# One step of a two-layer RWKV-7 and differential-attention trunk: the order of small products in quarters of the array, of the output projection, and of the memory keys

## The chip, the core and the metric

The kernel is one program on one core of a Trainium2 chip. The metric is the device time of one execution in microseconds (us). The engines are named as in the profile: PE (matrix products) and PEld (its weight loads), DVE (vector), ACT (scalar, activations and copies), POOL (general), SP (which issues the DMAs here). Each engine works through its own queue in order; semaphores tie the queues together.

## What is computed

Layer 0 mixes tokens with RWKV-7, layer 1 with differential attention. Each layer is a norm, one input projection, a mixer, a cross-attention over 256 memory rows (4 heads), a gate, one output projection and a residual add. Shapes: 512 prompt tokens and 32 sample tokens (544 columns in all), width 1024, 24 RWKV heads of 64, branch width 2048. All in float32.

```python
def rwkv_layer(x, mk, mv, prev_row, S0, norm_w, w_out, w_in, ...):
    h = rmsnorm(x, norm_w)
    p, qm, gate = jnp.split(h @ w_in, [RW_PROJ, RW_PROJ + MEM_W], axis=-1)
    y_mix, S_T, last_row = rwkv_mixer(p, prev_row, S0, ...)
    y_mem = mem_attention(qm, mk, mv)
    out = jnp.concatenate([y_mix, y_mem], axis=-1) * jax.nn.silu(gate)
    return x + out @ w_out, S_T, last_row

# in rwkv_mixer, for every token:
    sa = jnp.einsum('bhvk,bhk->bhv', S, -kk_t)
    S = S * w_t[:, :, None, :] + sa[..., None] * (kk_t * a_t)[:, :, None, :] + v_t[..., None] * k_t[:, :, None, :]
    y = jnp.einsum('bhvk,bhk->bhv', S, r_t)
# then a group norm of y per head, plus sum(r * k * r_k) * v
```

Layer 1 has the same frame, with `diff_layer` in the mixer's place. For each layer the memory rows are also normed and multiplied by `w_mem_k` and `w_mem_v` (outputs too).

## The kernel before

**Projections.** Activations lie with the feature on the 128 partitions and the 544 tokens along the free axis. A float32 product is made of three single-pass ones: activation and weight are each split into a rounded part and a rest (`hh`/`hl`, `whi`/`wlo`), and `hh*whi`, `hl*whi`, `hh*wlo` are summed in PSUM (tile `ps_g`). I call these *main products*; one takes 128 x 272. A weight block is 1024 x 128: `load` issues two DMAs into `raw` (5 buffers), `split` lets ACT make `whi` and DVE `wlo` (2 buffers each), and 48 main products use it. Products of plain float32 tiles (all others) appear in the trace as two records each, transposes as one.

**Layer 0** works on 12 pairs of heads. For each pair: `rw_prep` (decays, scaled keys, the 64 x 64 triangles `at` of nine chunks: eight of 64 tokens, and the sample), `rw_invert` on POOL (inverts 32 x 32 triangles, 62 small instructions, after a round trip through DRAM), `rw_back` and `rw_at` (the inverses come back by DMA), `rw_merge` (two rounds of sixteen 32 x 32 products, tile `ps_w`, join the inverses to 64 x 64), `rw_values` (64 x 64 products, tile `ps_v`), the recurrence `rw_chain` (23 steps, each a product `ps_c`, then DVE or ACT, then the next), `rw_outputs` (`ps_yc`), and `rw_finish` (the group norm `fin`: sums, square on ACT, an inverse root by eight small DVE instructions, five transposes `ps_y`, the gate, then a DMA of the gated block `sg` to the scratch tensor `oscr`).

**Order in layer 0.** It is written by hand. `Queue.tie` makes every engine keep the order in which the program names its instructions, while `ordered` is set. `FILL0` to `FILL3` give the opening (pairs 0 to 2 prepared between main products). Then for each pair `PLAN` has 23 rows of two halves: after each step of the recurrence it names what else is issued there, for the pair itself (0), the next (1), the ones after (2, 3) or the last (-1). Main products of the `blocks` list fill in between (192 in a usual pair). ACT and DVE work for the weight blocks waits in `later` and is issued one piece at a time by `some`. `MPLAN` does the same for the steps of the memory cross-attention in pairs 10 and 11.

**End of layer 0.** After pair 11's recurrence, its `rw_outputs` and `rw_finish` stand between the main products of `w_mem_k` of layer 1. Then `ordered` is off, and the framework's scheduler orders the rest: `w_out` fetches sixteen gated blocks from `oscr` into `os`, splits each into `hi` (ACT) and `lo` (DVE), and multiplies: eight output blocks `k`, each with two weight blocks `q`, each with two token halves, 24 main products in each. The residual comes in as products of raw rows of `x` with the identity into the same PSUM tile (`extra`, 48 products). ACT copies the sum to `x1` and squares it. `token_rms` and eight rounds of DVE, ACT and POOL (`hn`, `hh`, `hl`) then give layer 1's normed input, while PE multiplies `w_mem_v`.

**PSUM pools:** `psg` 3 banks (main products), `psm` 2, `psx` 1, `psc` 2 (recurrence).

**Layer 1** goes over 12 heads in three groups, with main products from `proj` and `gate`, and then `w_out` again, with the gated blocks in SBUF (`og`).

Of the kernel before, what the change touches and what calls it, by code (L numbers as in the profile page):

```python
# [2 lines left out]

# [5 lines left out]
F32 = mybir.dt.float32  # L9
# [7 lines left out]
P = 128  # L17
D = 1024
# [20 lines left out]
OSB = 4  # L39
# [4 lines left out]
LATER = 0.75  # L44
PLAN = [
    [[("val", 0, 1.1, 0), ("prep", 2, 0.1, 0)], [("prep", 2, 0, 0.42)]],
    [[("val", 0, 0.8, 0)], []],
    [[("prep", 1, 0.53, 0)], [("prep", 1, 0, 0), ("prep", 2, 0, 1.04)]],
    [[("prep", 2, 0.56, 1.0)], [("prep", 2, 0, 0)]],
    [[("smp", 0, 0.11, 0.28), ("prep", 1, 0.4, 0)], [("prep", 2, 0, 1.0)]],  # L50
    [[("out", -1, 0.11, 0), ("prep", 2, 0, 0.86)], [("prep", 2, 0, 0.84)]],
# [14 lines left out]
    [[("prep", 3, 0.33, 0), ("mrg", 1, 0.9, 0)], [("prep", 3, 0.33, 0), ("fin", -1, 0, 0.73)]],  # L66
# [3 lines left out]
MPLAN = {10: [(0, 0), (3.5, 0), (5, 0), (6, 0), (6.5, 1), (7, 0), (8, 0), (9, 0), (10, 0), (10.5, 0), (11, 0), (12, 0), (12.5, 1),  # L70
# [3 lines left out]
             + [(10.5 + k, 4) for k in range(10)]}  # L74

FILL0 = [8, 4, 8, 2, 2, 2, 2, 2, 6, 2, 14, 2, 4, 6, 6, 2, 6, 6, 6, 8, 16, 8, 6, 14, 2, 2, 2, 2, 2, 2, 2, 2]
FILL1 = [6, 14, 14, 2, 2, 2, 2, 2, 8, 2, 10, 2, 2, 6, 8, 2, 6, 6, 6, 8, 18, 8, 6, 10, 2, 2, 2, 2, 2]
FILL2 = [4, 6, 10, 2, 2, 2, 4, 4, 6, 2, 2]
FILL3 = [12, 4, 2, 2]
# [19 lines left out]
class Trunk:  # L99
# [391 lines left out]
    def rw_prep(self, st, rkv):  # L491
# [61 lines left out]
        pst = self.psm.tile([P, 512], F32, tag="m", name="ps_rt")  # L553
# [42 lines left out]
        k2 = k  # L596
        self.ve.tensor_tensor(k2[:], k[:], kf[:], ALU.mult)
# [10 lines left out]
        for q in range(2):  # L608
# [36 lines left out]
        st["bv"] = bv = self.rb.tile([P, T], F32, tag="bv", name="bv", bufs=4)  # L645
        for s in range(2):
# [4 lines left out]
            self.te.matmul(psq[:, :TH], self.hblk[:], rkk[:, h], start=True, stop=True)  # L651
# [71 lines left out]
    def rw_merge(self, st):  # L723

        at, p = st["at"], self.rb
# [9 lines left out]
        for e, (u, w) in enumerate(rows):  # L735
            for b in range(8):
# [6 lines left out]
        for e, (u, w) in enumerate(rows):  # L743
            for b in range(8):
# [14 lines left out]
    def rw_values(self, st):  # L759

        avz, H = self.avz, self.H
        for cs in ((0, 8), (1, 3, 5, 7), (2, 4, 6)):
            yield
            ps = self.psm.tile([P, 4, P], F32, tag="m", name=f"ps_v{cs[0]}")
            for j, c in enumerate(cs):
                e, zs, ro, A, cv, _ = self.place(st, c)
                for h in range(2):
                    self.te.matmul(ps[zs, j, H[h]], A[0][ro, h, :], cv[ro, H[h]], start=True, stop=True)
            i = slice(0, 5, 4) if cs[0] == 0 else slice(cs[0] // 2, 4)
# [957 lines left out]
```

## Time and profile before

| | |
|---|---|
| three timed runs | 1506.65, 1508.87, 1511.67 us, median 1508.87 us |
| the profiled execution | 1505.41 us, its span 1503.7 us |
| mean granted clock of PE in it | 0.985 |
| instructions in the span | 32159 |
| HBM read and written | 110.98 MB and 22.78 MB |

Span times run from the first to the last instruction. In a timeline row the first number is the start, the second the duration; a product's duration holds its way through the array, so the pace of a row of products is read from the start of one row to the start of the next. In a window row the columns are the window, its length, and for each engine its busy time and number of instructions; then the granted clock of PE, the DMA share and GB/s.

### The profile page before, as it was taken

How to read it: one execution, taken by the hardware profiler on the slowest of the kernel's cores; microseconds unless marked ns; L12 is line 12 of the kernel's file. 1: busy time of each engine (PE TensorE's matmuls, PEld its weight loads, DVE VectorE, ACT ScalarE, POOL GpSimd, SP SyncE). 2: the span in 40 equal slices, each digit the busy share in tenths (PEclk: the TensorE clock that was granted, in tenths of full speed). 3: DMA queues.
4: the chain of work that ended last, by engine and by line, in shares of the span. 5: the costliest groups of instructions: out<-in, count | busy, mean ns of one | idle time of the engine just before them, and what ended most of it. 6: DMA issues, size and time to landing. Idle time of an engine off the chain costs nothing.

```text
span 1503.7 us, 32159 instructions
## 1 busy us (share of the span) xinstructions
PE 1437.1 (96%) x12112; PEld 1347.2 (90%) x12112; DVE 897.8 (60%) x2223; ACT 824.4 (55%) x2257; POOL 379.5 (25%) x843
## 2 busy tenths in 40 slices
PE   5999999999999998999899989999999999999997
PEld 5988899999999997888789989899989999998997
DVE  7565677778777877566742264555355644447543
ACT  6655566766676666556542245663465544664322
POOL 2045557644575446600000040000001000100000
PEclk9999999999999999999999989999999999999999
DMA  6442222232222221423573352332333222332221
GB/s 220 128 113 76 58 53 63 74 90 70 68 68 74 76 71 47 115 62 101 165 217 101 90 151 86 91 89 79 99 85 86 82 85 78 86 91 83 78 85 67
DMA packets 266534, 139.22 MB, mean 93 GB/s; under 512 B 57658, under 2 KB 256579, under 8 KB 266379
## 3 DMA queue, kind: packets, MB, share of 16 engines
q1 hardware_dynamic: 266378, 137.16, 32.1%
q8 instruction: 96, 1.57, 0.4%
q14 instruction: 60, 0.48, 0.1%
HBM read 110.98 MB, written 22.78 MB: 89 GB/s over the span
## 4 chain that ended last, share of the span: by engine, by line
PE 78%; DVE 6%; ACT 5%; DMA 4%; POOL 4%; issue 2%; SPq 2%; DVEq 0%; ACTq 0%; POOLq 0%
PE ps_g L96 54%; PE ps_c L96 4%; PE ps_s L96 2%; PE ps_o L96 2%; PE ps_v L96 2%; POOL u L700 2%; SPq L96 2%; POOL tm L698 2%; PE ps_at L96 1%; PE ps_w L96 1%; PE ps_mm L96 1%; PE ps_mo L96 1%; DVE wlo L96 1%; ACT whi L96 1%; PE ps_aT L96 1%
## 5 line engine op out<-in xcount | busy, mean ns | idle before, releaser
L96 PE MATMUL ps_g<-hh,whi 128*128 128x272 f32 x1808 | 544.9, 301 | 0.1
L96 PE MATMUL ps_g<-hh,wlo 128*128 128x272 f32 x1808 | 538.9, 298 | 0.8 <-DVE wlo L96 0.8
L96 PE MATMUL ps_g<-hl,whi 128*128 128x272 f32 x1808 | 539.0, 298 | 0.0
L96 DVE TENSOR_TENSOR wlo<-raw,whi 128x512 fp32r<-128x512 f32 x322 | 223.7, 705 | 249.1 <-ACT whi L96 244.9
L96 PEld LDWEIGHTS ps_g<-hh,whi 128*128 128x128 f32 x1808 | 345.7, 191 | 4.5 <-issue 0.6
L96 PEld LDWEIGHTS ps_g<-hh,wlo 128*128 128x128 f32 x1808 | 344.2, 190 | 5.4 <-DVE wlo L96 1.2
L96 PEld LDWEIGHTS ps_g<-hl,whi 128*128 128x128 f32 x1808 | 344.3, 190 | 3.8
L96 ACT CAST whi<-raw 128x512 fp32r<-128x512 f32 x322 | 195.0, 617 | 220.6 <-PE ps_g L96 161.7
L698 POOL TENSOR_TENSOR tm<-u,m 102x84 f32<-102x84 f32 (+23 forms) x372 | 161.3, 434 | 204.3 <-DMA m<-sc 176.2
L700 POOL TENSOR_TENSOR u<-u,tm 102x84 f32<-102x84 f32 (+23 forms) x372 | 152.7, 411 | 29.1
L96 PE MATMUL ps_g<-hi,whi 128*128 128x272 f32 x512 | 150.2, 296 | 4.3 <-ACT hi L96 4.3
L96 PE MATMUL ps_g<-lo,whi 128*128 128x272 f32 x512 | 149.8, 294 | 1.9 <-DVE lo L96 1.9
L96 PE MATMUL ps_g<-hi,wlo 128*128 128x272 f32 x512 | 149.1, 292 | 0.2 <-DVE wlo L96 0.2
L1560 POOL TENSOR_TENSOR kz<-k,kh 64x544 fp32r<-64x544 f32 x24 | 32.6, 1359 | 419.4 <-ACT kh L96 418.4
L96 PEld LDWEIGHTS ps_g<-hi,whi 128*128 128x128 f32 x512 | 97.8, 192 | 6.1 <-ACT hi L96 5.6
L96 PEld LDWEIGHTS ps_g<-lo,whi 128*128 128x128 f32 x512 | 98.0, 192 | 3.8 <-DVE lo L96 3.7
L96 PEld LDWEIGHTS ps_g<-hi,wlo 128*128 128x128 f32 x512 | 98.1, 192 | 0.4 <-DVE wlo L96 0.4
L96 DVE SCALAR_TENSOR_TENSOR SB<-ps_c,dl,sd 64x64 f32<-64x64 f32 x168 | 47.5, 283 | 68.2 <-PE ps_c L96 42.4
L1442 POOL TENSOR_TENSOR hl<-hn,hh 128x544 fp32r<-128x544 f32 x8 | 11.9, 1523 | 237.7 <-ACT hh L96 237.7
L96 ACT ACTIVATE pt<-ps_s,snm 128x128 f32<-128x128 f32 (+3 forms) x96 | 50.7, 530 | 22.3 <-DVE snm L96 21.9
L96 ACT COPY raw<-ps_g 128x272 f32<-128x272 f32 x74 | 28.6, 387 | 56.7 <-PE ps_g L96 56.3
L96 DVE TENSOR_REDUCE snm<-ps_s 128x1 f32<-128x128 f32 (+3 forms) x96 | 46.1, 488 | 19.9 <-PE ps_s L96 17.8
(362 smaller groups left out, 2613.4 us busy)
## 6 DMA issues: line engine op xcount, KB each, us to landing
raw<-in_rw_in_dram SPq DMA_DIRECT2D x114, 256.0 KB
raw<-in_df_in_dram SPq DMA_DIRECT2D x112, 256.0 KB
raw<-in_w_out_dram SPq DMA_DIRECT2D x64, 256.0 KB
m<-sc SPq DMA_DIRECT2D x36, 128.0 KB
oscr<-sg SPq DMA_DIRECT2D x16, 272.0 KB
os<-oscr SPq DMA_DIRECT2D x16, 272.0 KB
raw<-in_w_mem_k_dram SPq DMA_DIRECT2D x16, 256.0 KB
raw<-in_w_mem_v_dram SPq DMA_DIRECT2D x16, 256.0 KB
```

The source lines that it names most:

```text
L96: return lambda *a, **k: self.trunk.tie(self, issue(*a, **k))
L698: nc.gpsimd.tensor_tensor(tm[:, :n, :wd], u3[:, :n, kx : kx + 1].to_broadcast(sh), m3[:, kx : kx + 1, kx + 1 :].to_broadcast(sh), ALU.mult)
L700: nc.gpsimd.tensor_tensor(u3[:, :n, kx + 1 :], u3[:, :n, kx + 1 :], tm[:, :n, :wd], ALU.add)
L1442: nc.gpsimd.tensor_tensor(self.hl[:, k, :], h[:], self.hh[:, k, :].bitcast(F32), ALU.subtract)
L1560: nc.gpsimd.tensor_tensor(kz[rows[m], m, :], k[rows[m], :], hi.bitcast(F32), ALU.subtract)
```

## The change

1. **Values, merges, outputs.** `rw_values` issues the first pair of chunks alone as before, then the odd and the even chunks together, one product of each by turns, into two PSUM banks; before they were two separate calls. The odd chunks use rows 64 to 127 and columns 0 to 63 of the array, the even ones rows 0 to 63 and columns 64 to 127. `rw_merge` alternates between its two 32 x 32 squares, `rw_outputs` between its two column halves. `PLAN` drops the third call of `rw_values`, moves the second round of a merge half a step later, and some steps of `rw_prep` earlier. The transpose `ps_rt` goes to the pool `psx`.
2. **r_k.** From pair 3 on, `rkk` is a plain product on POOL instead of DVE; ACT scales the block of ones (`hb`) by `r_k` instead.
3. **Pairs 9 to 11.** Main products: pair 9 takes 144 instead of 96 (a memory query moves into it), pairs 10 and 11 take 192 instead of 240; the gate of pair 11 comes after the last pair. `mem_again` leaves pair 11.
4. **End of layer 0.** `w_out` becomes a generator and starts during pair 11's `rw_finish` (`TAIL`), with the queues still in written order. Output blocks 0 and 1 go together over groups of four gated blocks, in four PSUM banks; block 11, the last to be gated, comes last. Gated blocks land directly in `lo`; odd ones get their `lo` on POOL. The residual is transposed into `ps_x`, copied to `x1` by ACT, and the product is added by DVE.
5. **Memory keys of layer 1** are multiplied after `token_rms`, together with the memory values, beside the norm of layer 1.
6. **Weights.** A list `ahead` of all later weight blocks; `used`, called after each block's products, splits the next block and loads one more.
7. Tiles are moved between pools, so that the output projection's memory is free earlier. The lists `FILL0` to `FILL3` and `MPLAN` have new numbers.

```diff
-    [[("val", 0, 1.1, 0), ("prep", 2, 0.1, 0)], [("prep", 2, 0, 0.42)]],
-    [[("val", 0, 0.8, 0)], []],
+    [[("val", 0, 0.95, 0), ("prep", 2, 0.1, 0)], [("prep", 2, 0, 0.42)]],
+    [[], [("prep", 2, 0, 1.04)]],
...
-    [[("prep", 3, 0.33, 0), ("mrg", 1, 0.9, 0)], [("prep", 3, 0.33, 0), ("fin", -1, 0, 0.73)]],
+    [[("prep", 3, 0.33, 0)], [("mrg", 1, 0.9, 0), ("prep", 3, 0.33, 0), ("fin", -1, 0, 0.73)]],
...
+TAIL = (("fin", 6), ("fin", 6), ("fin", 6), ("fin", 6), ("rsq", 6), ("split", 6), ("split", 6), ("split", 6), ("fin", 6),
+        ("split", 6), ("fin", 6), ("fin", 6), ("out", 6))
...
+    def used(self):
+
+        if self.early:
+            w, todo = self.split(self.early.pop(0))
+            for fn, _ in todo:
+                fn()
+            self.made.append(w)
+        if self.ahead:
+            self.early.append(self.load(*self.ahead.pop(0)))
...
-                self.ve.scalar_tensor_tensor(rkk[:], r[:], col(self.rk), k2[:], ALU.mult, ALU.mult)
+                spare.tensor_tensor(rkk[:], r[:], k2[:], ALU.mult)
+                hb = p.tile([P, P], F32, tag="hb", name="hb", bufs=1)
+                self.ae.activation(hb[:], self.hblk[:], AF.Copy, scale=col(self.rk))
...
-        for e, (u, w) in enumerate(rows):
-            for b in range(8):
+        for b in range(8):
+            for e, (u, w) in enumerate(rows):
                 self.te.matmul(ps[w, b * 32 : b * 32 + 32], ab[e][u, b, B[1]], t1[u, b, :], start=True, stop=True)
...
-        for cs in ((0, 8), (1, 3, 5, 7), (2, 4, 6)):
+        for sets in (((0, 8),), ((1, 3, 5, 7), (2, 4, 6))):
             yield
...
+            ps = [self.psm.tile([P, 4, P], F32, tag="m", name=f"ps_v{cs[0]}") for cs in sets]
+            for j in range(len(sets[0])):
                 for h in range(2):
...
+                    for q, cs in zip(ps, sets):
+                        if j < len(cs):
+                            _, zs, ro, A, cv, _ = self.place(st, cs[j])
+                            self.te.matmul(q[zs, j, H[h]], A[0][ro, h, :], cv[ro, H[h]], start=True, stop=True)
...
+    def gated(self, g, hi, lo, t):
+
+        self.ae.copy(hi[:], t)
+        (self.nc.gpsimd if g % 2 else self.ve).tensor_tensor(lo[:], t, hi[:].bitcast(F32), ALU.subtract)
+        return hi, lo
...
+        half = [[g for g in order if g // 8 == q] for q in range(2)]
+        units = [(k, q, half[q][4 * j : 4 * j + 4], j == 1) for q in range(2) for j in range(2) for k in range(2)]
+        units += [(k, q, half[q], True) for k in range(2, KT) for q in range(2)]
...
+            for k, q, gs, last in units:
+                if (k, q) not in ws:
+                    ws[k, q] = self.weights(None, 0)
+                hi, lo = ws[k, q]
+                ahead(len([g for g in gs if g not in o]))
...
+            def residual(k, vs):
...
+                        self.te.transpose(ps[:, c - o : c - o + r.stop - r.start], xs[k][r, c // P, :], self.ident[r, r])
+                    self.ae.copy(self.x1[:, k, v], ps[:, v.start - o : v.stop - o])
...
+            def consume(k, ps, v):
+                x = self.x1[:, k, v]
+                self.ve.tensor_tensor(x, ps, x, ALU.add)
+                self.square_sums((k, x, v), p, sums)
...
+            for kind, n in TAIL:
+                if kind == "split":
+                    ahead(1)
+                else:
+                    go(kind, NPAIR - 1)
+                fill2(n)
...
+            kv = chain(*(self.mem_kv(1, mh, ml, kind, self.psm, "m") for kind in range(2)))
```

Here `fill2(n)` issues n main products of what is left (first the gate of pair 11, then the output projection).

Three places show the new order, engine by engine. The first is PE, around the change from pair 7 to pair 8: `ps_yc` are the outputs of pair 7, `ps_v` the values of pair 8, `ps_c` the recurrence, `ps_g` main products. Before:

```order
L96 MATMUL ps_yc<-sv,at_89 64x64 x16
L96 MATMUL ps_g<-hh,wlo 128x272
L96 MATMUL ps_c<-avz,at_1775 128x128
L96 MATMUL ps_v_7913<-sv,at_1775 64x64 x8
L96 MATMUL ps_rt<-ident,rr 128x128
L96 MATMUL ps_g<-hh,whi 128x272
L96 MATMUL ps_g<-hl,whi 128x272
L96 MATMUL ps_g<-hh,wlo 128x272
L96 MATMUL ps_g<-hh,whi 128x272
L96 MATMUL ps_c<-sv,bt 128x128
L96 MATMUL ps_v_7948<-sv,at_1775 64x64 x6
```

Now:

```order
L102 MATMUL ps_yc<-sv,at_91 64x64 x16
L102 MATMUL ps_g<-hh,wlo 128x272
L102 MATMUL ps_c<-avz,at_1782 128x128
L102 MATMUL ps_v_7921<-sv,at_1782 64x64
L102 MATMUL ps_v_7922<-sv,at_1782 64x64
L102 MATMUL ps_v_7921<-sv,at_1782 64x64
L102 MATMUL ps_v_7922<-sv,at_1782 64x64
```

The eight and the six products stand in one place now, by turns, ahead of the recurrence's next product.

The second place is PE, around the second round of pair 8's merge (`ps_w` from `wm`) and the first values products of that pair. Before:

```order
L96 MATMUL ps_wa<-lora_663,uz 128x272
L96 MATMUL ps_w_7830<-at_1775,wm 32x32 x16
L96 MATMUL ps_wa<-lora_663,uh 128x272
L96 MATMUL ps_wa<-lora_663,uz 128x272
L96 MATMUL ps_g<-hh,wlo 128x272
L96 MATMUL ps_g<-hh,whi 128x272
L96 MATMUL ps_c<-avz,at_89 128x128
L96 MATMUL ps_v_7864<-sv,at_1775 64x64 x2
```

Now:

```order
L102 MATMUL ps_wa<-lora_672,uz 128x272
L102 MATMUL ps_g<-hh,whi 128x272
L102 MATMUL ps_g<-hl,whi 128x272
L102 MATMUL ps_g<-hh,wlo 128x272
L102 MATMUL ps_w_7842<-at_1782,wm 32x32 x16
L102 MATMUL ps_wa<-lora_672,uh 128x272
L102 MATMUL ps_wa<-lora_672,uz 128x272
L102 MATMUL ps_c<-avz,at_91 128x128
L102 MATMUL ps_v_7874<-sv,at_1782 64x64 x2
```

Three main products moved ahead of the merge's second round, and two fewer stand between it and the values that read its result.

The third place is POOL, where one pair's inversion ends (`u`, `tm`) and the next begins (`CAST`). Now:

```order
L720 TENSOR_TENSOR tm<-u_5315,m_5308 102x11
L722 TENSOR_TENSOR u_5315<-u_5315,tm 102x11
L646 TENSOR_TENSOR rkk<-rkv 128x544
L714 CAST u_6059<-ui 102x352
L720 TENSOR_TENSOR tm<-u_6059,m_6052 102x31
```

Before, nothing stood between the end of one inversion and the `CAST`; the `rkk` of a later pair now stands there.

More of the change, by code (lines that the diff above doesn't have):

```diff
@@ L2 @@
 from contextlib import ExitStack
+from itertools import chain
 import concourse.bass as bass
@@ L841, in rw_outputs @@
         ps = self.psx.tile([P, 4, P], F32, tag="x", name="ps_yc")
-        for c in range(8):
-            self.outputs(st, c, ps, c // 2)
+        for i in range(4):
+            self.outputs(st, (2 * i, 2 * i + 1), ps, i)
         self.ve.tensor_tensor(yt[:, :4, :], ps[:], yt[:, :4, :], ALU.add)
@@ L976, in mem_kv @@
         src, out = self.mem_source(i, kind)
+        last = None
         for h in range(MH):
@@ new lines, in w_out, with fetch, ahead, products @@
+    def w_out(self, i, p, order, consume, extra=None):
+        came, o = [], {}
+        left = list(order)
+        def fetch():
+            if left:
+                g = left.pop(0)
+                came.append((g, self.fetch(p, g)))
+        def ahead(n):
+            for _ in range(n):
+                if came:
+                    g, t = came.pop(0)
+                    o[g] = self.gated(g, *t)
+                    fetch()
+        for _ in range(NGATED):
+            fetch()
+        half = [[g for g in order if g // 8 == q] for q in range(2)]
+        units = [(k, q, half[q][4 * j : 4 * j + 4], j == 1) for q in range(2) for j in range(2) for k in range(2)]
+        units += [(k, q, half[q], True) for k in range(2, KT) for q in range(2)]
+        ws, ps = {}, {}
+        halves = [slice(0, TH), slice(TH, T)]
+        def products():
+            for k, q, gs, last in units:
[3 more added lines that the diff above has]
+                ahead(len([g for g in gs if g not in o]))
+                if q == 0 and k not in ps:
+                    pool, tag = (self.psc, "c") if k == 1 else (self.psg, "g")
+                    ps[k] = [pool.tile([P, 512], F32, tag=tag, name="ps_g") for _ in range(2)]
+                end = q == 1 and last
+                for vs in [halves] if k < 2 else [[v] for v in halves]:
+                    for j, g in enumerate(gs):
+                        if k < 2 and (j + k) % 2 == 0:
+                            ahead(1)
+                        if end and extra is not None and j == len(gs) // 2:
+                            extra(k, vs)
+                        for v in vs:
+                            out = ps[k][v.start // TH][:, :TH]
+                            wh, wl = hi[:, g % 8, :], lo[:, g % 8, :]
+                            for x, y in ((wh, o[g][0]), (wh, o[g][1]), (wl, o[g][0])):
+                                self.te.matmul(out, x, y[:, v], start=q == 0 and g == half[0][0] and x is wh and y is o[g][0],
+                                                 stop=end and g == gs[-1] and x is wl)
+                                yield
+                    if vs[-1].stop == T and last:
+                        self.used()
+                    if end:
+                        for v in vs:
+                            consume(k, ps[k][v.start // TH][:, :TH], v)
+        return products(), ahead
@@ L1338, in layer0 @@
                 load = [HOPV[k % 3] + sum(us for x in y for kind, d, _, us in x if 0 <= pr + d < NPAIR) for k, y in enumerate(PLAN)]
-                step = (sum(took) + MEMPE * len(mplan) / 12 + MAIN * each[pr]) / len(PLAN)
+                whole = sum(took) + MEMPE * len(mplan) / 12 + MAIN * each[pr]
+                pace = [max(x, 1.4) for x in load] if each[pr] < 3 * 6 * KT else [1.0] * len(PLAN)
+                due = [whole * sum(pace[:k]) / sum(pace) for k in range(len(PLAN) + 1)]
                 room = (sum(load) + 2.3 * each[pr] / 48) / len(PLAN)
@@ L1359, in layer0 @@
                                 t += MEMPE / 12
-                        spent += self.some(room * (k + (half + 1) / 2) + 0.4 - spent)
-                        while left and t + MAIN / 2 < step * (k + (half + 1) / 2):
+                        if FULL not in x:
+                            spent += self.some(room * (k + (half + 1) / 2) + 0.4 - spent)
+                        while left and t + MAIN / 2 < (due[k + 1] if half else (due[k] + due[k + 1]) / 2):
                             next(main)
@@ L1509, in consume @@
                         self.ve.tensor_tensor(ys[i][n, :512], pf[n, :], fw[n, :512], ALU.mult)
-            self.w_out(1, po, list(range(8)) + [12, 13, 14, 15, 8, 9, 10, 11], consume)
+            for _ in self.w_out(1, po, list(range(8)) + [12, 13, 14, 15, 8, 9, 10, 11], consume)[0]:
+                pass
             rs = self.token_rms(sums, p)
@@ L1679, in run @@
         self.wp = self.pool("w", 1)
-        self.gp = self.pool("gate", 1)
+        gp = self.pool("gate", 1)
+        self.sg, self.gates = [gp.tile([P, T], F32, name=f"sg{i}") for i in range(SGB)], 0
         self.rctx = ExitStack()
```

296 lines of the change are left out of this document (162 added, 134 removed), and 6 rows, old and new, of the table MPLAN.

## The prediction

> **What bounds the kernel now.** I read the first part of the page, then the chain that ended last.
>
> ```profile
> PE 1437.1 (96%) x12112; PEld 1347.2 (90%) x12112; DVE 897.8 (60%) x2223; ACT 824.4 (55%) x2257; POOL 379.5 (25%) x843
> PE 78%; DVE 6%; ACT 5%; DMA 4%; POOL 4%; issue 2%; SPq 2%; DVEq 0%; ACTq 0%; POOLq 0%
> ```
>
> PE is busy for 96% and carries 78% of the chain; DVE and ACT are used a little over half. So a change gains either where PE stands idle or where PE's own instructions go through in less time. The average hides the stages, so I cut the span at the outputs (`ps_yc`) of pairs 4, 5, 8, 9, 10 and 11, and at the edges of the output projection and of layer 1's norm.
>
> ```profile
> 383.00:430.80 47.80, 47.28 (x469) 44.53 (x466) 36.66 (x91) 32.79 (x94) 26.47 (x61) 1.00 0.28 74
> 576.20:614.80 38.60, 34.50 (x356) 30.77 (x355) 29.63 (x77) 22.64 (x71) 21.17 (x53) 1.00 0.21 51
> 614.80:672.10 57.30, 54.92 (x500) 51.48 (x499) 33.51 (x85) 33.15 (x103) 17.11 (x46) 1.00 0.33 92
> 672.10:729.70 57.60, 55.26 (x432) 50.00 (x431) 36.98 (x95) 31.45 (x98) 0.00 (x0) 1.00 0.31 95
> 729.70:768.40 38.70, 32.62 (x236) 28.72 (x235) 25.01 (x47) 19.82 (x38) 0.00 (x0) 0.91 0.76 232
> 768.40:864.20 95.80, 95.80 (x776) 95.80 (x776) 25.53 (x44) 27.17 (x61) 0.00 (x0) 1.00 0.39 114
> 864.20:899.00 34.80, 28.54 (x210) 27.46 (x209) 22.90 (x52) 16.60 (x37) 16.84 (x14) 0.90 0.48 141
> 1388.00:1392.00 4.00, 1.89 (x8) 1.45 (x9) 4.00 (x9) 4.00 (x8) 0.00 (x0) 0.89 0.88 260
> ```
>
> A usual pair (first row) leaves PE idle for 47.80 - 47.28 = 0.5 us: there, only cheaper products help. Pair 9 (second row) idles 4.1, pairs 10 and 11 idle 2.4 and 2.3. The sixth row, the dense output projection, gives the price of a main product: 95.80 / 776 = 0.1235 us. The stages ahead of and behind it (fifth and seventh rows) are where PE waits; their clock is 0.91 and 0.90. So three things can give: the small products of twelve pairs, the unevenness of pairs 9 to 11, and the two edges.
>
> **Values.** In PE's timeline, pair 6's values stand in a row of sixteen records and one of twelve; each is timed from its start to the next row's.
>
> ```profile
> 431.40 1.14 PE L96 MATMUL ps_v<-sv,at 64*64 64x64 f32 x16
> 432.47 0.33 PE L96 MATMUL ps_rt<-ident,rr 128*128 128x128 f32 x1
> ...
> 433.46 0.91 PE L96 MATMUL ps_v<-sv,at 64*64 64x64 f32 x12
> 434.30 0.39 PE L96 MATMUL ps_g<-hl,whi 128*128 128x272 f32 x1
> ```
>
> Sixteen take 1.07 and twelve 0.84 us, 1.91 together or 0.07 a record: one quarter of the array works at a time. With two quarters by turns and two banks, the longer row (1.07) can cover the shorter one; left is 1.0 to 1.1. I take 0.85 off each of twelve pairs: -10.2 us (bounds 5 and 11; the wider end is 12 x 0.91, the narrower one if turns overlap only half).
>
> **Merges.** The first round of a merge, and its records counted in two windows of 0.16 us, in the middle of the first square and around its change to the second:
>
> ```profile
> 418.67 1.09 PE L96 MATMUL ps_w<-t1b,at 32*32 32x32 f32 x32
> 419.69 0.40 PE L96 MATMUL ps_g<-hh,wlo 128*128 128x272 f32 x1
> ...
> 418.91:419.07 0.16, 0.16 (x11) 0.16 (x9) 0.00 (x0) 1.00 0.24 64
> 419.07:419.23 0.16, 0.16 (x14) 0.16 (x12) 0.00 (x0) 1.00 0.12 35
> ```
>
> A round takes 1.02 us for 32 records, 0.032 each. Around the change, 14 records are in flight in the window instead of 11, so the second square does start while the first still works. If turns get a round to 0.65, two rounds save 0.7 a pair: -8.4 us over twelve pairs (0 if the squares exclude each other; 10 if a round halves, less the edges). [...]
>
> **The wait ahead of the merge's second round.** It shows in the list of waits; behind it comes the copy that the first values need.
>
> ```profile
> PE ps_w L96 <- DVE bv L96: 4.6, 10, 0.9
> ...
> 426.54 0.39 PE L96 MATMUL ps_wa<-lora,uh 128*128 128x272 f32 x1
> ...
> 426.64 0.74 ACT L96 COPY at<-ps_w 32x256 f32<-32x256 f32 x2 [1.07 <-PE ps_w L96]
> ```
>
> The second round now stands behind three more main products (3 x 0.1235 = 0.37), against 0.46 a wait, so most of the 4.6 us go. But the first values product now follows it by two main products instead of four, and the copies end at 426.64 + 0.74 = 427.38, 0.84 after the round. Two main products and a step of the recurrence cover about 0.5; 0.35 x 11 = 4 us are lost again. Net 0, bounds -4 and +4.
>
> **Residual.** The 48 identity products become 48 transposes, which have one record instead of two; ACT copies and DVE adds lie beside PE. Five identity records, and four transposes of the same width:
>
> ```profile
> 863.75 0.65 PE L96 MATMUL ps_g<-ident,xr 128*128 128x112 f32 x5
> 864.24 0.58 PE L96 MATMUL ps_n<-ones,sums 128*128 128x1 f32 x4
> ...
> 435.63 0.60 PE L96 MATMUL ps_v<-ident,rkv 128*128 128x128 f32 x4
> 435.99 0.37 PE L96 MATMUL ps_g<-hh,whi 128*128 128x272 f32 x1
> ```
>
> 0.49 / 5 = 0.098 a record before, 0.36 / 4 = 0.09 now: 96 x 0.098 - 48 x 0.09 = 5.1 us, less some 0.11 for each of sixteen changes from main products and back (1.8): -3.3 us (0 to 4).
>
> **Pairs 9 to 11.** The sum of main products is the same; pair 9 gets 48 more, pairs 10 and 11 48 fewer, and 48 (the last gate) come behind them. What can go is their idle time above a usual pair's: 3.6 + 1.9 + 1.8 = 7.3 us. I take -6 (2 to 8).
>
> **Opening of the output projection, and layer 1's norm.** The two edge windows again, with main products alone:
>
> ```profile
> 729.70:768.40 38.70, 30.67 (x189) 26.48 (x189) 0.44 (x1) 1.88 (x5) 0.91 0.76 232
> 864.20:899.00 34.80, 26.41 (x182) 24.68 (x180) 0.70 (x2) 3.72 (x10) 0.90 0.48 141
> ```
>
> At the opening 189 main products are worth 189 x 0.1235 = 23.3 us and the 47 others some 2.6: 38.7 - 25.9 = 12.8 us are lost, mostly while pair 11 is gated and its block goes out and in. Now 42 gate and 24 output products stand ahead of the transposes `ps_y` and 132 behind them, enough for that chain. But DVE's chain gets longer by the `lo` splits put into it, two of which took 1.41 us:
>
> ```profile
> 749.76 1.41 DVE L96 TENSOR_TENSOR lo<-os,hi 128x544 fp32r<-128x544 f32 x2 [1.17 <-ACT hi L96]
> ```
>
> I leave 5 of the 12.8: -7.8 us (2 to 10). In the norm stage 182 x 0.1235 = 22.5 and 28 x 0.1 = 2.8 leave 34.8 - 25.3 = 9.5 lost. The memory keys' 96 main products come there now and leave the opening, which is 0 in itself, and fill it. But `wlo` must come in time, and DVE slows beside POOL:
>
> ```profile
> 869.50 0.68 DVE L96 TENSOR_TENSOR wlo<-raw,whi 128x512 fp32r<-128x512 f32 x1
> ...
> 879.43 6.25 DVE L96 TENSOR_TENSOR wlo<-raw,whi 128x512 fp32r<-128x512 f32 x4
> ...
> 874.58 10.55 POOL L1442 TENSOR_TENSOR hl<-hn,hh 128x544 fp32r<-128x544 f32 x7 [0.26 <-ACT hh L96]
> ```
>
> A `wlo` takes 0.68 alone and 6.25 / 4 = 1.56 while POOL makes `hl`. I leave 3.5 of the 9.5: -6 us (2 to 8). Before layer 1's output projection PE idles 4.00 - 1.89 = 2.1 us (last row of the stages); the list `ahead` has its weights ready: -2 (0 to 3).
>
> **The r_k product on POOL, and other moves.** `rkk` leaves DVE and now stands in POOL's queue between an inversion and the next `CAST`:
>
> ```profile
> 449.45 0.77 DVE L96 SCALAR_TENSOR_TENSOR rkk<-rkv,PA 128x544 f32<-128x544 f32 x1
> ...
> 447.55 0.23 POOL L700 TENSOR_TENSOR u<-u,tm 102x11 f32<-102x11 f32 x1
> 451.39 0.48 POOL L692 CAST u<-ui 102x352 f32<-102x352 bf16 x1 [3.61 <-DMA sc<-u]
> 463.39 0.24 POOL L698 TENSOR_TENSOR tm<-u,m 102x31 f32<-102x31 f32 x1 [11.52 <-DMA m<-sc]
> ```
>
> POOL has 3.61 us there, and 11.52 behind; at the 1.51 us of an `hl` (10.55 / 7) the product fits. DVE's 9 x 0.77 lie off the path. With the nine `hb`, the moved prefetches and new fill numbers I take 0, bounds -5 and +8, since any of them can bring a wait for a weight block.
>
> **Sum.** -10.2 - 8.4 + 0 - 3.3 - 6 - 7.8 - 6 - 2 + 0 = -43.7 us. The profiled execution took 1505.4 us (span 1503.7 and 1.7 around it), 3.5 under the median 1508.9: 1461.7 by its time, 1465 by the median.
>
> **The rivals.**
>
> *Merges gain nothing.* Both squares write one PSUM tile from different rows of the array; if their writes exclude each other, the 8.4 stay: 1473. For it: no row has squares by turns. Against it: 14 records against 11. [...] Chance 0.12.
>
> *The pairs do not get shorter.* With 18.6 us less product time, the 23 steps of the recurrence, each a product and then DVE or ACT, could bind instead of PE, and idle time in a pair rise from 0.5 to 2: 1465 + 18.6 = 1484. For it: pair 9, with 96 main products instead of 192, saved 9.2 us and not 96 x 0.1235 = 11.9. Against it: that pair still shows a recurrence can pass in 38.6 us, and a usual pair stays at 46. Chance 0.12.
>
> *More stalls go.* If the opening's 5, the norm's 3.5, the last 1.3 of pairs 9 to 11 and the 4 of the copies go too: 1465 - 13.8 = 1451. For it: all of PE's waits there have main products beside them now. Against it: the `lo` and `wlo` rows. Chance 0.10.
>
> *It comes to nothing.* Neither turns nor edges give, since quarters don't overlap and the last group norm's chain ends later by what was covered: 1509. Against it: two separate causes would have to fail. Chance 0.04.
>
> *Slower: the inversions come late.* `rkk` waits in POOL's queue for `rkv`, and the inversion waits behind it. SP's and DVE's rows for the inverses' return and the merge that reads them:
>
> ```profile
> 456.47 1.93 SPq L96 DMA_DIRECT2D at<-sc  x4
> 458.95 2.08 SPq L96 DMA_DIRECT2D m<-sc  x6
> ...
> 465.95 0.90 DVE L96 STREAM_TRANSPOSE t1b<-at 32x256 f32<-32x256 f32 x2
> ```
>
> The issue of `m` ends at 461.03 and POOL reads it at 463.39, so a landing takes about 2.4; `at` is back at 458.40 + 2.4 = 460.8, 5.1 us before it is read. An inversion later by more than that delays each of nine pairs. It becomes slower than now from 5.1 + (43.7 + 4.5) / 9 = 10.5 us on; at 11 us, 9 x 5.9 = 53 less 43.7 gives +9: 1518. For it: SP's queue and POOL's are both in written order. Against it: DVE had `rkv` at 449.45, 2 us before the `CAST`. Chance 0.04.
>
> **How the numbers follow.** Forecast 0.58, its own range 1452 to 1480: the terms' bounds taken as independent (root of the summed squares, 15 up and 10 down, and some 3 for the runs' spread of 1506.65 to 1511.67 either way). To hold 8 in 10, the range takes in the pair rival at 1484 with a part of its spread, and the 1451 case: 1450 to 1489. About 0.3% of this kernel, 4.5 us, can be told from no change. Faster by more: 0.58 + 0.12 + 0.12 + 0.10 = 0.92; same 0.04; slower 0.04.
>
> **What would show it.** [...] The forecast is wrong if the sum of twelve pairs does not fall by some 20 us, or if a wait of PE for `wlo`, `lo` or `at` over 5 us in total stands in the list that isn't there now.

## The result and the profile after

The changed kernel takes 1473.15 us (median of four runs, 1470.78 to 1475.02); the kernel before takes 1507.76. The ratio is 0.9765, 95% interval 0.9739 to 0.9792. The gain of 35 us is four fifths of the 44 that were forecast, and 1473 lies in the forecast's own range (1452 to 1480). It also happens to be the time of the first rival ("merges gain nothing"), which experiment 2 rules out. One execution of the kernel of experiment 9 took 1544.63 us at a granted clock of 0.835; it and its profile are left out.

The first part of the page after, and then the windows of a usual pair, of pairs 9, 10 and 11, and of the stretch behind pair 11:

```profile
PE 1411.7 (96%) x12064; PEld 1326.1 (90%) x12064; DVE 899.0 (61%) x2214; ACT 826.1 (56%) x2269; POOL 421.3 (29%) x868
```

```profile
375.80:421.90 46.10, 45.60 (x467) 42.96 (x466) 36.20 (x90) 33.21 (x95) 29.51 (x64) 1.00 0.29 76
560.90:603.30 42.40, 38.49 (x402) 35.15 (x401) 31.96 (x80) 25.93 (x77) 27.09 (x67) 1.00 0.26 65
603.30:656.00 52.70, 47.93 (x451) 44.15 (x450) 31.28 (x81) 31.01 (x99) 12.47 (x37) 1.00 0.33 90
656.00:704.60 48.60, 46.72 (x377) 42.49 (x376) 31.04 (x81) 26.20 (x88) 0.00 (x0) 1.00 0.25 73
704.60:741.90 37.30, 33.36 (x251) 31.24 (x251) 25.00 (x41) 16.07 (x30) 12.01 (x8) 0.91 0.74 233
```

PE's busy time fell by 25 us; it is as bound as before. A usual pair is 1.7 us shorter at the same idle time (0.5): its products got cheaper. Pairs 9, 10 and 11 idle 3.9, 4.8 and 1.9 us, 10.6 together, more than the 8.8 before.

The two profiled executions (spans 1503.7 and 1473.2, so 30.5 us of the 35 can be placed) laid side by side by stage, at marks that both have. Main products that moved between stages are taken out at 0.125 us; in the dense rows now, 23 of them take 2.87 us. The 0.1235 of the forecast was an average that held the residual's shorter identity products.

| stage | before | after | moved products | net | forecast |
|---|---|---|---|---|---|
| start to pair 0's outputs | 187.9 | 191.5 | 0 | +3.6 | -1.6 |
| pairs 1 to 8 | 388.3 | 369.4 | 0 | -18.9 | -12.4 |
| pairs 9 to 11 | 153.5 | 143.7 | -48 | -3.8 | -10.7 |
| to the sums of the norm (`ps_n`) | 134.6 | 123.3 | -49 | -5.2 | -11.1 |
| norm, to the first head of layer 1 | 44.5 | 53.7 | +95 | -2.7 | -6.0 |
| layer 1 | 595.0 | 591.6 | 0 | -3.4 | -2.0 |

The sum is right to a fifth by the medians, and these two executions reach 70% of it. That it came so near is in part luck: the usual pairs and layer 1 gave more than asked, four other places gave less, and about 3 us of what the usual pairs gave is the clock of these two executions (below). What PE waits for, in the list of waits after:

```profile
PE ps_w L102 <- DVE t1b L102: 8.9, 6, 4.5
...
PE ps_ckT L102 <- DMA ck<-in_cache_k_dram: 4.9, 1, 4.9
PE ps_g L102 <- DVE lo L102: 3.6, 3, 2.0
PE ps_g L102 <- ACT hi L102: 3.5, 2, 2.0
...
PE ps_ck L102 <- DMA cmt<-in_cache_mem_k_dram: 2.2, 1, 2.2
...
PE ps_w L102 <- DVE bv L102: 0.2, 1, 0.2
```

The wait for `bv` (4.6 before) is gone. On top stands one that the forecast did not have: the merge's first round waits for the transposes `t1b`, 7.8 of the 8.9 us in the opening and 1.1 in pair 9. Since `t1b` is the inverses (`at`) transposed, the sign that the forecast named for being wrong, over 5 us of new waits for `wlo`, `lo` or `at`, is there in substance. Of the waits for `lo` and `hi`, 2.0 us each stand ahead of layer 1's output projection, the rest ahead of layer 0's.

**The small products.** Values, a merge's first round and its second round in PE's timeline of two usual pairs, each with the row that follows:

```profile
423.61 1.14 PE L102 MATMUL ps_v<-sv,at 64*64 64x64 f32 x28
424.68 0.33 PE L102 MATMUL ps_rt<-ident,rr 128*128 128x128 f32 x1
...
457.83 0.99 PE L102 MATMUL ps_w<-t1b,at 32*32 32x32 f32 x32
458.75 0.39 PE L102 MATMUL ps_g<-hl,whi 128*128 128x272 f32 x1
...
464.57 0.69 PE L102 MATMUL ps_w<-at,wm 32*32 32x32 f32 x32
465.19 0.40 PE L102 MATMUL ps_wa<-lora,uh 128*128 128x272 f32 x1
```

Values take 1.07 us instead of 1.91. The two rounds, both 1.02 before, now differ: 0.92 and 0.62. The turns in `rw_outputs`, which the forecast gave no term, are worth little: its 32 records take 1.08 us instead of 1.12.

**The opening of layer 0.** PE at the start of pair 0's first merge round, SP's queue before it, and the window behind it:

```profile
138.57 0.31 PE L102 MATMUL ps_w<-t1b,at 32*32 32x32 f32 x2 [4.49 <-DVE t1b L102]
```

```profile
130.77 1.11 SPq L102 DMA_DIRECT2D up<-in_rw_w_up_dram  x2
131.92 1.23 SPq L102 DMA_DIRECT2D up<-in_rw_a_up_dram  x2
133.20 1.14 SPq L102 DMA_DIRECT2D raw<-in_rw_in_dram  x2
134.38 1.98 SPq L102 DMA_DIRECT2D at<-sc  x4
...
136.90 2.32 SPq L102 DMA_DIRECT2D m<-sc  x6
```

```profile
138.60:148.00 9.40, 9.25 (x122) 8.33 (x123) 1.75 (x6) 5.09 (x16) 4.80 (x17) 0.59 0.43 119
```

PE stands 4.5 us for the return of the first inverses (`at`), which SP issues behind three loads that can wait (experiment 11); then the clock is 0.59 for 9.4 us. The wait costs twice: the clock drops 2.0 us into the wait of 4.5 us and is 0.50 from 136.1 to 146.3 us. The wait ahead of pair 1's first merge round is only 2.6 us, yet a stretch at half clock follows it too:

```profile
180.40:187.20 6.80, 6.72 (x55) 6.66 (x56) 2.99 (x14) 3.05 (x10) 2.47 (x10) 0.50 0.60 165
```

That this wait sets it off is not shown: in the kernel before, PE waits only 0.4 us at that place, and the clock is 0.50 from 176.0 to 182.8 us.

In the kernel before, the same three loads stood ahead of the return, and PE waited only 0.2 us for it. Both kernels have 664 main products ahead of that place. But PE now comes to it at 134.1 us instead of 137.0, mostly because two waits of 1.2 and 1.5 us on the way are gone, and the inversion starts 2.1 us later. The first step of the inversion, before and after:

```profile
94.71 0.24 POOL L698 TENSOR_TENSOR tm<-u,m 102x31 f32<-102x31 f32 x1 [55.08 <-DMA m<-sc]
```

```profile
96.84 0.24 POOL L720 TENSOR_TENSOR tm<-u,m 102x31 f32<-102x31 f32 x1 [56.48 <-DMA m<-sc]
```

It waits for the triangles `m`, which SP issues at nearly the same time in both kernels (90.36 and 90.61 us); a weight load now goes out just ahead of them. That this load delays their landing was not tried.

**The start of layer 1.** The cached keys' first transposes, as a window around them:

```profile
866.40:876.80 10.40, 5.54 (x25) 5.57 (x26) 3.05 (x8) 2.90 (x7) 0.11 (x1) 0.67 0.65 174
```

Again idle time (4.9) and then a low clock (0.67 over the window).

### The profile page after: what moved, and what is told of

Its sections match the earlier page's. It is cut to its first block, busy times and chain, and to the rows that moved or that the text cites. A ratio compares the mean times of both kernels' runs of the same rounds, so it can differ in the third digit from the quotient of the medians.

```text
span 1473.2 us, 32147 instructions
## 1 busy us (share of the span) xinstructions
PE 1411.7 (96%) x12064; PEld 1326.1 (90%) x12064; DVE 899.0 (61%) x2214; ACT 826.1 (56%) x2269; POOL 421.3 (29%) x868
## 4 chain that ended last, share of the span: by engine, by line
PE 84%; DVE 6%; ACT 4%; DMA 3%; issue 2%; SPq 1%; DVEq 0%; ACTq 0%
PE ps_g L102 58%; PE ps_c L102 4%; PE ps_s L102 3%; PE ps_o L102 2%; PE ps_at L102 2%; PE ps_v L102 2%; PE ps_mm L102 1%; SPq L102 1%; DVE wlo L102 1%; PE ps_mo L102 1%; PE ps_ss L102 1%; PE ps_w L102 1%; PE ps_aT L102 1%; PE ps_yc L102 1%; PE ps_kv L102 1%
## 5 line engine op out<-in xcount | busy, mean ns | idle before, releaser
L720 POOL TENSOR_TENSOR tm<-u,m 102x84 f32<-102x84 f32 (+23 forms) x372 | 155.3, 417 | 183.3 <-DMA m<-sc 155.2
L722 POOL TENSOR_TENSOR u<-u,tm 102x84 f32<-102x84 f32 (+23 forms) x372 | 163.6, 440 | 29.1
L102 ACT COPY sv<-ps_c 64x64 f32<-64x64 f32 x192 | 39.3, 205 | 38.9 <-PE ps_c L102 37.1
L102 ACT ACTIVATE sg<-ps_g 128x272 f32<-128x272 f32 x64 | 25.2, 394 | 51.0 <-PE ps_g L102 50.7
```

Source lines behind the costliest of these rows:

```text
L102: return lambda *a, **k: self.trunk.tie(self, issue(*a, **k))
L720: nc.gpsimd.tensor_tensor(tm[:, :n, :wd], u3[:, :n, kx : kx + 1].to_broadcast(sh), m3[:, kx : kx + 1, kx + 1 :].to_broadcast(sh), ALU.mult)
L722: nc.gpsimd.tensor_tensor(u3[:, :n, kx + 1 :], u3[:, :n, kx + 1 :], tm[:, :n, :wd], ALU.add)
```

## The experiments

Each ran in five rounds beside the kernel before; its ratio to that kernel is given. The changed kernel's is 0.9765, so a difference has to be about 0.003 (4.5 us) before it can be told from none. Edits are to the changed kernel, except in the fifth.

**1. Values in a row.**

```diff
-            for j in range(len(sets[0])):
-                for h in range(2):
-                    for q, cs in zip(ps, sets):
-                        if j < len(cs):
+            for q, cs in zip(ps, sets):
+                for j in range(len(cs)):
+                    for h in range(2):
```

> The changed kernel, with the odd chunks' values first and the even chunks' after them, in the same place and banks, no longer by turns. Theory A (turns halve PE's own time, and the pairs are bound by PE): the row of 28 value records goes from 1.07 back to about 1.9 us, each usual pair from 46.1 to 46.9 us, the whole kernel 10 us (0.7%) slower than the changed one, so 1483. Rival B (pairs are bound by the recurrence, not by PE's products): the row gets longer but PE idles less, and the kernel stays within 2 us of 1473.

Measured: 1477.06 us, ratio 0.9806 (0.9790 to 0.9823), 6 us over the changed kernel's ratio, though the two intervals just touch; the row itself is the firmer evidence. The values of pair 6 there:

```profile
424.71 1.66 PE L102 MATMUL ps_v<-sv,at 64*64 64x64 f32 x28
426.31 0.33 PE L102 MATMUL ps_rt<-ident,rr 128*128 128x128 f32 x1
```

The row is 1.60, not 1.9. Theory A holds with another size: the turns are worth 0.53 a pair, 12 x 0.53 = 6.4. The other 0.31 of the 0.84 came from putting both sets in one place. About half of it is the start and the end of a row, which are paid once instead of twice (in the kernel before, the first two records of a row start 107 ns apart, the next ones 58, and from the last one to the next row it is 152). At this pace 28 records in one row would take 107 + 26 x 58 + 152 = 1767 ns; the 0.17 us that are left to 1.60 are, by my estimate, an overlap at the change of sets. In the kernel before, three records at the change of a merge's squares start 5 to 6 ns behind the ones before them; for the sets themselves it was not shown.

**2. Merges in a row.**

```diff
-        for b in range(8):
-            for e, (u, w) in enumerate(rows):
+        for e, (u, w) in enumerate(rows):
+            for b in range(8):
```

(in both rounds)

> The changed kernel, with each round of a merge going through one square and then the other, as before the change. Theory A (turns work in one PSUM bank, but the first round now also waits for the second DVE transpose): the second round goes from 0.62 back to 1.02 us, the first from 0.92 to 1.02, a usual pair from 46.1 to 46.6, the kernel 6 us slower, 1479. Rival B (row tiles that write one bank exclude each other, the rounds get shorter for another reason): rounds keep 0.92 and 0.62, the kernel stays at 1473 within 2. Rival C (the prediction's 0.35 a round): 8.4 us slower, 1481.

Measured: 1479.74 us, ratio 0.9829 (0.9813 to 0.9846). The second round in its timeline, and one of its pairs as a window:

```profile
372.40 1.09 PE L102 MATMUL ps_w<-at,wm 32*32 32x32 f32 x32
373.42 0.40 PE L102 MATMUL ps_wa<-lora,uh 128*128 128x272 f32 x1
```

```profile
376.10:423.70 47.60, 47.56 (x469) 45.21 (x468) 36.06 (x90) 33.31 (x96) 30.73 (x68) 0.96 0.29 75
```

The rounds are 1.02 again, so turns within one PSUM tile do work, and the rival "merges gain nothing" falls: squares on different rows of the array write one PSUM tile by turns at 0.62 / 32 = 0.019 us a record, against 0.032 in a row. Rounds account for 6 us (0.1 and 0.4 in twelve pairs). The time rose by 6.6 us by the medians and by 9.6 by the ratios, whose intervals leave some 5 us of play, so 6 fits. Two of this profile's pairs ran at a clock of 0.96 and were 1.2 us longer with no wait that the list shows; in the changed kernel's profile it was one.

**3. Transposes half a step earlier.**

```diff
-    [[("prep", 3, 1.04, 0.17)], [("mrg", 1, 0, 0.86)]],
+    [[("mrg", 1, 0, 0.86), ("prep", 3, 1.04, 0.17)], []],
```

> The changed kernel, with the two DVE transposes of a merge issued half a step earlier, ahead of a small square root step and one weight split. Theory A (the first round stalls 0.25 us after two records because its second product by turns needs the second transpose): the gap goes, the first round takes 0.65 to 0.7 instead of 0.92, and ten usual pairs together give 2 to 2.5 us: 1471. Rival B (the gap is PE's own, not a wait): the round stays at 0.92 and the time at 1473.

Measured: 1466.48 us, ratio 0.9737 (0.9721 to 0.9753), at the edge of what the times can show.

```profile
454.26 0.69 PE L102 MATMUL ps_w<-t1b,at 32*32 32x32 f32 x32
454.89 0.40 PE L102 MATMUL ps_g<-hl,whi 128*128 128x272 f32 x1
```

The round takes 0.63, as the second one does. The 0.3 was the wait for the second transpose: in a row, the first square's sixteen records had covered it; by turns, the third record needs it (it starts 0.26 us behind the second one in the changed kernel's profile). Usual pairs fell from 46.1 to 45.6 us, more than the round's 0.3; where the other 0.2 came from was not settled.

**4. Half of the first inversion left out.**

```diff
-        for kx in range(31):
+        for kx in range(31 if st["pr"] else 15):
```

> The changed kernel, but the inversion of pair 0 alone leaves out 32 of its 62 POOL instructions, so that its result comes some 13 us earlier. Theory A (the opening of layer 0 is bound by the first two inversions, not by PE): PE's waits of 4.8 and 2.9 us ahead of the first rounds of the merges of pairs 0 and 1 go, with the lower clock behind them; the end of pair 0 moves from 191.5 to 184 or earlier and the kernel is 7 us faster, 1466. Rival B (PE is held up there by something else, such as the landing of a DMA issued in order): the end of pair 0 moves by less than 2 us, 1472.

Measured: 1467.47 us, ratio 0.9741 (0.9726 to 0.9756), less of a difference than the times can show. PE at the first merge round of pair 0 and of pair 1:

```profile
135.08 0.91 PE L102 MATMUL ps_w<-t1b,at 32*32 32x32 f32 x32
...
174.77 0.31 PE L102 MATMUL ps_w<-t1b,at 32*32 32x32 f32 x2 [3.88 <-DVE t1b L102]
175.73 1.05 PE L102 MATMUL ps_w<-t1b,at 32*32 32x32 f32 x30 [0.65 <-DVE t1b L102]
```

The first wait is gone, and the second has grown from 2.6 to 3.9 us: half of theory A. The opening is held by the inversions, but pair 1's does not start earlier because pair 0's ends earlier. Pair 0's outputs come at 186.4. In other profiles with the changed kernel's opening they came between 188.8 and 191.5; the +3.6 of the table is at the high end of that.

**5. The kernel before, with turns alone.** Values of both sets in the second call, merges by turns, the third call empty, `ps_rt` in the other pool.

> The kernel before, with the turns alone: values of the odd and the even chunks together in one place, merges by turns, nothing else moved (the third call for values is left empty, the small transpose of pair preparation goes to the other pool). Theory A (pairs are bound by PE's own instructions): a usual pair falls from 47.8 by 0.84 for the values and 0.5 for the two merge rounds to about 46.5; twelve pairs give 16 us, 1491. Rival B (half of the pairs' gain comes from the moved order and the waits that it removed): a usual pair stays above 47.2, the kernel at 1499 or above.

Measured: 1494.36 us, ratio 0.9933 (0.9907 to 0.9958). A usual pair, and the waits that grew:

```profile
281.40:328.20 46.80, 45.76 (x467) 43.04 (x466) 36.57 (x91) 32.95 (x95) 29.39 (x66) 1.00 0.29 75
```

```profile
PE ps_w L96 <- DVE bv L96: 5.8, 10, 1.4
PE ps_at L96 <- DVE bk L96: 5.5, 10, 1.7
```

Between the theories: PE is busy for 1.5 us less in a pair, its idle time rises from 0.5 to 1.0, and the pair falls by 1.0. Without the moved steps the waits for `bv` and `bk` take a part of the gain: both grew (4.6 and 4.7 us before), where in the changed kernel they are 0.2 and 0.9. So about 1 of the 1.7 us of a pair is turns; the other 0.7 is what remains for the moved steps and the rest of the change.

**6. Loads of pair 1's triangles first.**

```diff
-                    go("at", 0)
                     go("inv", 1)
+                    go("at", 0)
```

> The changed kernel; in the opening, SP issues the loads of pair 1's triangles before the return of pair 0's inverses instead of behind it. Theory A (the second wait of the opening is pair 1's inversion, which starts late only because its loads stand behind the return in SP's queue): the inversion of pair 1 starts about 5 us earlier, the wait of 1 to 3 us ahead of pair 1's first merge round goes with its lower clock, pair 0 ends at 187 to 188 instead of 190 to 191.5, the kernel gains 3 us: 1468. Rival B (the loads were not what held it): pair 0 ends no earlier than 189.5, no change within 1.5.

Measured: 1473.39 us, ratio 0.9787 (0.9757 to 0.9816); pair 0's outputs at 190.9.

```profile
139.90 0.31 PE L102 MATMUL ps_w<-t1b,at 32*32 32x32 f32 x2 [5.72 <-DVE t1b L102]
```

A failed; the time and pair 0's end are those of rival B. The inversion of pair 1 started at 139.5 us instead of 141.9, not 5 us earlier. The second wait fell to 0.9 us, but it is 1.0 in experiment 1 too, whose opening is unchanged. The first rose from 4.5 (3.3 to 4.8 in the other profiles with this opening) to 5.7: I had counted on room in SP's queue, and the loads `up` and `raw` (3.5 us in the rows above) fill it. What moves ahead there pushes the return back.

**7. Cached keys transposed later in layer 1.** The four transposes `ps_ckT` and their copy go behind the first head's three projections.

> The changed kernel; the first four transposes of layer 1, of cached keys, are written behind the first head's three projections instead of ahead of them. Theory A (at the start of layer 1, PE stands 4.9 us for the landing of cached keys that are queued behind weight loads, and then runs 6.8 us at half clock): both go, 5 us and about 3 us, 1464 to 1465. Rival B (the weights would be late at that place too, and PE waits for these instead): 0 to 2 us.

Measured: 1463.64 us, ratio 0.9726 (0.9698 to 0.9755), some 6 us under the changed kernel's ratio: theory A, with 6 of its 8 us. The place where PE had stood:

```profile
866.00:876.00 10.00, 9.83 (x81) 8.99 (x80) 5.44 (x12) 7.00 (x18) 0.00 (x0) 1.00 1.03 249
```

PE is busy 9.83 of 10 us and the clock stays at 1.00.

**8. Pair 10's cached memory keys a step later.**

```diff
-MPLAN = {10: [(0, 0), (1, 0), (2, 0), (3, 0),
+MPLAN = {10: [(0, 0), (2, 0), (2, 0), (3, 0),
```

> The changed kernel; in pair 10 the transposes of the first cached memory keys stand one step of the recurrence later. Theory A (pairs 9 to 11 did not get shorter because the moved steps wait for transfers that were given one step to land, 2.4 us at this place): pair 10 goes from 52.6 to about 50.5 and the kernel gains 2 us, 1471. Rival B (pair 10 is bound by the recurrence and the other work, the wait only stands where slack is): pair 10 stays at 52.5, no gain.

Measured: 1468.78 us, ratio 0.9762 (0.9733 to 0.9792): no difference that the times can show. The window of pair 10:

```profile
600.90:652.20 51.30, 48.06 (x452) 44.13 (x450) 31.42 (x81) 31.15 (x100) 13.41 (x39) 1.00 0.34 92
```

The wait for the cached memory keys fell from 2.2 to 0.2 us. The pair is 1.4 us shorter and still idles 3.2: the moved step's transfer was part of it, less than theory A's 2.

**9. Pairs 9 and 10 as before.** The first memory query goes back to pair 10, with the old steps of its memory attention.

> The changed kernel; the first memory query stands in pair 10 again, so that pair 9 takes 96 main products and pair 10 takes 240, with the steps of pair 10's memory attention as before the change. The prediction (evening out the three pairs takes most of their idle time): 5 to 6 us slower than the changed kernel, 1476. Rival B (the evening out gave nothing, since the moved steps brought waits of their own, 2.4 us for cached memory keys among them): pairs 9 and 10 together take the same 95 us within 1.5, 1470 to 1472.

Measured: 1467.92 to 1472.68 us, ratio 0.9764 (0.9743 to 0.9784), the changed kernel's own but for 0.0001: rival B. Evening out pairs 9 and 10 gave nothing that the times can show. Pair 11 was not put back, and where the idle time stands in this kernel stays open.

**10. All rests on DVE.**

```diff
-        (self.nc.gpsimd if g % 2 else self.ve).tensor_tensor(lo[:], ...
+        self.ve.tensor_tensor(lo[:], ...
```

> The changed kernel with all rests of the gated blocks computed by DVE, none by POOL, in both output projections. Theory A (the openings are bound by DVE's chain with splits and weight rests, and POOL takes half of the splits off it): the opening of layer 0's output projection gets 2 to 3 us longer, layer 1's as well, 1475. Rival B (POOL's slower splits and its contention with DVE cost what they save): no change or 1 to 2 us faster, 1469.

Measured: 1469.53 us, ratio 0.9758 (0.9736 to 0.9779): rival B. POOL's share of the splits neither gains nor loses. PE's waits at these places:

```profile
PE ps_g L102 <- ACT hi L102: 3.0, 2, 2.0
PE ps_g L102 <- DVE lo L102: 2.4, 3, 1.1
```

They are no longer than with POOL (3.5 and 3.6), at layer 0's place (1.1 and 1.3 us, with POOL 1.5 and 1.6) as at layer 1's.

**11. Four orders mended together.** Experiments 3, 7 and 8, and in the opening:

```diff
             go("back", 0)
+            go("inv", 1)
+            go("at", 0)
             for k, n in enumerate(FILL2):
...
-                if k == 3:
-                    go("at", 0)
-                    go("inv", 1)
```

> The changed kernel with four orders mended together: the merges' transposes half a step earlier, layer 1's cached-key transposes behind the first projections, pair 10's cached memory keys a step later, and in the opening both the loads of pair 1's triangles and the return of pair 0's inverses ahead of the other loads in SP's queue. Theory A (these waits are separate places on the path, each with half-clock time behind it): 5 + 6 + 1.5 + 3 = 15 us under the changed kernel, 1456, and the first wait of the opening falls from about 5 to about 3 us, the second goes. Rival B (what one gives, the next wait takes back, as with the loads of pair 1 alone): 1461 or above.

Measured: 1451.39 us (1450.75 to 1454.19), ratio 0.9639 (0.9619 to 0.9658): 1.3% under the changed kernel. SP's queue in the opening, PE at pair 0's first merge round, and the clock behind it:

```profile
129.70 1.98 SPq L102 DMA_DIRECT2D m<-sc  x6
131.72 1.79 SPq L102 DMA_DIRECT2D at<-sc  x4
...
134.12 1.11 SPq L102 DMA_DIRECT2D up<-in_rw_w_up_dram  x2
```

```profile
134.27 0.24 PE L102 MATMUL ps_w<-t1b,at 32*32 32x32 f32 x2
134.93 0.69 PE L102 MATMUL ps_w<-t1b,at 32*32 32x32 f32 x30 [0.41 <-DVE t1b L102]
```

```profile
136.00:148.00 12.00, 11.17 (x135) 10.28 (x133) 6.23 (x15) 10.17 (x29) 10.04 (x26) 1.00 0.52 143
```

The return goes out 2.7 us earlier, the first wait is down to 0.4 us, the clock stays at 1.00, and pair 0's outputs come at 182.2, 7 to 9 us earlier than with the changed kernel's opening. More than A's sum: by the ratios 19 us instead of 15, and the opening gave 7 to 9 where A had 3. A wait of 4.5 us was worth more than itself, since the half clock went with it: the opening from 134 us on has 3.4 us at half clock now instead of 17.1.

**12. As 11, with 18 main products of the opening moved behind pair 0's triangles.**

> As the kernel before in this list, and 18 main products of the opening stand behind the triangles of pair 0 instead of ahead of them. Theory A (the opening is bound by the chain of pair 0's inversion from its triangles on, and PE's products there have slack): POOL starts 2.3 us earlier, the first wait falls by as much, pair 0 ends 2 to 3 us earlier, 1453 to 1454. Rival B (the triangles wait for DVE and ACT, not for PE's place in order): PE idles ahead of the triangles instead, no gain within 1 us.

Measured: 1453.34 us, ratio 0.9646 (0.9627 to 0.9665); pair 0's outputs at 182.1 against 182.2. POOL did start 2.2 us earlier (93.73 us instead of 95.91), and yet A failed: PE idles 1.2 us ahead of the triangles and begins the merge at 135.6 instead of 134.3, now without a wait. With the queue mended, the triangles' place no longer matters.

## Why the prediction was right, and where its steps failed

- **Values** (-0.85 a pair): right, 0.84. The reason was half of it: turns gave 0.53, the common place 0.31.
- **Merges** (-0.35 a round): the mechanism was right, the size not: 0.1 and 0.4 instead of 0.35 twice. The step "if turns get a round to 0.65" held for the second round; the first then needs both transposes at once, which experiment 3 shows.
- **The wait ahead of the second round** (net 0): the old wait went as worked out, 4.4 of 4.6 us, but the new one at the copies did not come; the 4 us lost in that step were never lost. In the profile after, the values start with no wait 0.67 us behind the second round, which is cover enough. This is one part of why pairs 1 to 8 gave 18.9 instead of 12.4: their idle time fell from 4.8 to 2.7 us. A larger part is the clock, and that part is luck: of the eight pairs before, three ran at 0.96 to 0.98 and took 1.2 to 1.5 us longer, of those after one (1.1), which makes 3.0. The rest of the excess lies in PE's busy time and was not taken apart.
- **The pair rival** (1484): it did not come; a usual pair idles 0.5 as before. Experiment 5 shows that it would have come in part without the moved steps.
- **Pairs 9 to 11** (-6): this step failed. Idle time above a usual pair's was taken for something that evening out removes. It belongs to waits of its own, and new ones came with the moved steps: in pair 10 the transfer that had one step to land (2.2 us, experiment 8), in pair 9 `t1b` and `avz` (1.1 each), `wlo` (0.7) and `bk` (0.6). Experiment 9 puts the gain of pairs 9 and 10 at none.
- **Residual** (-3.3): mis-sized. The transposes stand in groups of three between main products:

```profile
756.25 0.54 PE L102 MATMUL ps_x<-ident,xr 128*128 128x128 f32 x3
756.72 0.39 PE L102 MATMUL ps_g<-hi,whi 128*128 128x272 f32 x1
756.95 0.29 PE L102 MATMUL ps_g<-lo,whi 128*128 128x272 f32 x1
```

  A group takes 0.47 us, 0.16 a transpose, and the main product behind it 0.23 instead of 0.125. At this price 48 take about 7.7 us against 9.4 for the old records: 1.7 at most, less with the edges. No part of the gain could be seen by itself.
- **Opening of the output projection** (-7.8): about -3.5 with the residual taken off the table's -5.2. Waits of PE for `hi` (1.5), `lo` (1.6) and `yt` (0.9) remain, 3.9 us of idle time in the window where there were 6.1, and so does the clock of 0.91. That DVE's splits bind it was my reason for leaving 5; experiment 10 speaks against it, and what makes these operands late stays open.
- **Norm stage** (-6): of the 9.5 us that I counted as lost, 3.1 were PE's wait for the cached keys, at the very end of my window, and no memory key can fill it: it stands behind all of them. This is the step that failed. The other 6.4 went entirely (the window of 38.5 us from `ps_n` on is full), but the wait grew from 3.1 to 4.9 us, and the half clock behind it from 3.4 to 6.8 us, worth some 1.7 more; that leaves about the 2.7 of the table. Rows of after and of before:

```profile
827.90:866.40 38.50, 38.50 (x315) 37.77 (x313) 26.60 (x56) 23.20 (x50) 16.59 (x14) 1.00 0.64 183
```

```profile
895.90:899.00 3.10, 0.02 (x1) 0.02 (x1) 1.43 (x5) 0.60 (x2) 0.40 (x1) 1.00 0.90 240
```

- **Layer 1** (-2): -3.4, for another reason. The idle time ahead of its output projection was a wait for `hi` and `lo` (1.9 and 1.2 us), which weights made ready earlier cannot shorten: it is 2.0 and 2.0 now. Short waits of the scores went, which in the list of before are these and in that of after are none over 0.2:

```profile
PE ps_s L96 <- ACT ssb L96: 2.3, 9, 0.3
...
PE ps_s L96 <- ACT pt L96: 1.7, 9, 0.2
```

- **rkk on POOL** (0): no wait in the list points to it in the usual pairs; it was not tried alone. The slower rival's mechanism, late inversions, did appear, though in the opening, where `rkk` is not on POOL, and through SP's queue.
- **What was missing**: the opening of layer 0. The forecast let its lists of fills pass as neutral. But PE came to the end of a chain (triangles, DRAM, inversion, DRAM) 3 us sooner while the chain started 2 us later, and waited there.
- **The range** (1452 to 1480): the bounds as given combine to 16 up and 8 down; with 3 for the spread that is 1454 to 1484. The result lies in either.

## What to carry to other kernels

When products are reordered by turns, look at what the second stream's operand waits for: what was hidden behind the first stream is now needed at once. When work on the bounding engine is made cheaper, look for the chain on the other engines that it had just covered; in a queue in written order, the cure here was to put the transfer on that chain ahead of loads that have time. Price a wait of PE of several microseconds with the half clock that comes with it (here 10.2 us of it with a wait of 4.5, 6.8 with one of 4.9), and ask of every wait inside a window whether the change reaches it: time that is lost in a window is not all of one kind.

## What the runs showed of the hardware

Two 32 x 32 squares on different rows and columns of the array, writing different partitions of one PSUM tile, overlap: 32 records in 0.62 us, against 1.02 in a row; by turns, the records of the two squares start 6 to 7 and 25 ns apart in alternation, in a row 31 to 32. Waits of PE of 4.5 and 4.9 us are each followed by a stretch at a granted clock of about half (0.59 over 9.4 us; 0.67 over 10.4 us with the wait in it), and so is a wait of 2.6 us (0.50 over 6.8 us). Where the wait of 4.5 us is down to 0.4 (experiment 11) and that of 4.9 us is gone (experiment 7), the clock stays at 1.00; at the place of the 2.6 us it was 0.50 over 6.8 us in the kernel before too, behind a wait of 0.4. Single usual pairs ran at 0.96 to 0.98 with no wait in the list to account for it, and took 1.1 to 1.5 us longer; what sets this off was not found.
